# Rotated query halves by ScalarE row copies, and positional scores as split products on stacked rows

## The chip, the cores and the metric

The kernel runs on one core of one Trainium2 chip. TensorE (PE in the profile) multiplies matrices and writes to PSUM; VectorE (DVE) and ScalarE (ACT) do the elementwise work; GpSimd (POOL) and SyncE (SP) hardly compute here, and SP issues nearly all transfers. The metric is device microseconds for one execution of the whole kernel, the median of several runs. All numbers are float32 in memory.

## The reference

Two encoder layers over 256 tokens of width 2048. Each layer has two groups of attention heads that share one input projection, an output projection, and an MLP. This case touches the second group, multi-head latent attention with 8 heads. A head's query and key have a content part of 128 columns and a positional part of 64, and the positional key is the same for all heads:

```python
def _rope(x, cos, sin):
    half = x.shape[-1] // 2
    x1, x2 = x[..., :half], x[..., half:]
    out = jnp.concatenate([x1 * cos - x2 * sin, x2 * cos + x1 * sin], axis=-1)
    return out.astype(x.dtype)
...
        q_rope = _rope(q[..., MLA_NOPE:], cos[:, :, None, :], sin[:, :, None, :])
...
        k_rope = _rope(kr, cos, sin)
...
        s = (jnp.einsum('bhqd,bhkd->bhqk', qn, knt)
             + jnp.einsum('bhqr,bkr->bhqk', qr, k_rope)).astype(jnp.float32) * scale
        p = jax.nn.softmax(s, axis=-1)
        return jnp.einsum('bhqk,bhkd->bhqd', p.astype(vt.dtype), vt)
```

A rotation needs each 64-column vector twice: as it is, and with its two halves of 32 exchanged.

## The kernel before

Activations lie transposed, features on the 128 rows (partitions) and the 256 tokens along the free dimension. A weight comes from memory as a "raw" tile, 1 MB at a time, and is split into a high part in the format float32r (`hi`, made by ScalarE, line 151) and the remainder (`lo`, a subtraction on VectorE, line 154). A product is then three float32r matmuls: high by high, high by low, low by high (`mac`, lines 191 to 198). Smaller products, among them all scores, are plain float32 matmuls, each of which the profile shows as two instructions.

A layer of attention (function `layer`, lines 867 to 1018) emits its work in this order: the combined projection; the differential heads' columns, mixed with their probabilities (`probs`); `up_k`, the latent keys; `up_q(0)`, the content queries of heads 0 to 3; `up_r`, the positional queries of all heads; `mla[0]`, the scores of head 0; `up_v`, the latent values; the scores of head 1 and the transpose of head 0; `up_q(1)`; and then, interleaved, the value columns of the differential heads (`val`, whose matmuls are lines 296 to 298) with the other latent heads: scores, transpose, values, each head one step behind the last. The output projection `w_o` follows.

`up_r` (line 924) makes two PSUM banks, each with four heads' positional queries: two pairs of heads side by side along the free dimension, and the two heads of a pair on rows 0 to 63 and 64 to 127. `copy` (line 346) moves a bank to the tile `qr`, scaled. `rope_q` (line 1218) then exchanges the halves of 32 rows by a product with a permutation matrix (128 columns of the constants `K`, at `C_PERM`), into the bank `pqr`, and combines both with cosine and sine on VectorE (lines 1225 to 1227). `rope_k` (line 1203) makes the positional key once a layer: the tile `kr` holds it twice, on rows 0 to 63 of its first half and on rows 64 to 127 of its second, with zeros elsewhere (a GpSimd memset, line 1212), so that one float32 product of all 128 rows picks out one head of the pair. `scores` (lines 1310 to 1321) runs, for each of two blocks of 128 tokens, a content product (line 1315) and a positional product (line 1316) into the bank `psm`; VectorE negates it and finds the extreme (line 1317), ScalarE takes the exponentials (line 1236) and scales by the reciprocal sum (line 1320).

What sets the order: the program's order is a priority only. A scheduler orders each engine's instructions when the kernel is built, by that priority and its own estimate of when operands and buffers will be ready; on the chip each engine then goes through its list in order. `behind` adds an order by hand where a line asks for it; none of the touched lines does. The pools bound the distance: 5 raw buffers, 4 each of `hi` and `lo`, 40 tiles of 128x512 in the pool `u`, 6 in the pool `t`, 8 PSUM banks. Beside all this run the modulation weights (`ada`): 192 tiles of 1 MB, loaded into raw buffers at a set rate and reduced by VectorE (line 380).

Of the kernel before, what the change touches and what calls it, by code (L numbers as in the profile page):

```python
# [9 lines left out]
F32 = mybir.dt.float32  # L10
F32R = mybir.dt.float32r
I32 = mybir.dt.int32
AF = mybir.ActivationFunctionType
ALU = mybir.AluOpType
AX = mybir.AxisListType

P = 128
# [20 lines left out]
]  # L38

C_DELTA = 0  # L40
C_PERM = 32
C_CB = 160
C_W2 = 168
C_FREQ = 176
C_SGN = 177
C_ONE = 178
NCONST = 180

V_BADA = 0
V_SUBLN = 192  # L50
# [19 lines left out]
def consts():  # L70
    c = np.zeros((P, NCONST), np.float32)
    p = np.arange(P)
    c[p, C_DELTA + p % 32] = 1.0
    c[p, C_PERM + (p ^ 32)] = 1.0
    for g in range(8):
        for r in range(4):
            b = 4 * g + r
            n = b % 16
            lo, hi = BUCKET_FROM[n], BUCKET_FROM[n + 1] - 1
            sign = -1.0 if b < 16 else 1.0  # L80
            rows = slice(32 * r, 32 * r + 32)
            if b == 16:
                c[rows, C_CB + g], c[rows, C_W2 + g] = 0.0, -1.0
            else:
                c[rows, C_CB + g] = -sign * (lo + hi) / 2.0
                c[rows, C_W2 + g] = ((hi - lo) / 2.0 + 0.25) ** 2
    c[:, C_ONE : C_ONE + 2] = 1.0
    c[:32, C_ONE + 1] = 0.0
    c[:, C_FREQ] = np.asarray(INV_FREQ, np.float32)[p % 32]
    c[:, C_SGN] = np.where(p % 64 < 32, -1.0, 1.0)  # L90
    return c
# [10 lines left out]
class Trunk:  # L102
# [308 lines left out]
    def setup(self):  # L411
# [8 lines left out]
        nc.gpsimd.memset(self.eps, EPS)  # L420
        self.K = cp.tile([P, NCONST], F32, name="K")
        nc.sync.dma_start(self.K, io["consts"])
# [119 lines left out]
    def bias_marks(self, a):  # L542
# [5 lines left out]
        for g in (2, 3, 6, 7, 0, 1, 4, 5):  # L548
            sq = self.t("sq")
            self.by_act.append(nc.scalar.activation(sq, r, AF.Square, bias=K[:, C_CB + g : C_CB + g + 1]))  # L550
            oh = half("oh", F32R)
            flat = sq.rearrange("p a b -> p (a b)")
            if g % 4 < 2:
                c = C_ONE + (g == 4)
                self.by_act.append(nc.scalar.activation(oh, flat, AF.Relu, bias=K[:, c : c + 1], scale=-1.0))
            else:
                w2 = K[:, C_W2 + g : C_W2 + g + 1]
                self.by_dve.append(nc.vector.tensor_scalar(oh, flat, w2, None, ALU.is_le))
# [20 lines left out]
    def rope_setup(self):  # L579
# [3 lines left out]
        self.behind(nc.vector.tensor_copy(ang, pos[:, :T]), self.last_mod)  # L583
        nc.vector.tensor_scalar(ang, ang, K[:, C_FREQ : C_FREQ + 1], None, ALU.mult)
        magic = 1.5 * 2.0**23
# [15 lines left out]
        nc.scalar.activation(self.cos, c, AF.Sin)  # L601
        nc.vector.tensor_scalar(self.sin, self.sin, K[:, C_SGN : C_SGN + 1], None, ALU.mult)

# [263 lines left out]
    def layer(self, l, acc=None):  # L867
        nc, io = self.nc, self.io
        qs = 1.0 / math.sqrt(128.0)
        ms = 1.0 / math.sqrt(192.0)  # L870
# [29 lines left out]
        cq, ckv = [], []  # L900
        kk, qn, kn, qr, vm, a, at, v, o = [], [], [], [], [], [], [], [], []
# [20 lines left out]
            qn.extend(self.copy(ps, "qn", ms) for ps in self.small(io["w_uq"][l, b], cq, 4))  # L922

        def up_r():
            raw = [self.copy(ps, "qr", ms) for ps in self.small(io["w_uq"][l, 2], cq, 4)]
            qr.extend(self.rope_q(x) for x in raw)

        def up_v():
            w = self.weights(io["w_uv"][l])
# [54 lines left out]
        up_q(0)  # L984
        turn(0)()
        up_r()
        turn(1)()
        mla[0]()
# [24 lines left out]
        o = self.mo + o  # L1013
# [11 lines left out]
        for fb in range(NFB):  # L1025
            hid = []
            done = 12 - 6 * l
            for m in range(0 if fb else done, NK, 2):
                srcs = [io[f"w_m1{l}"][NK * fb + m + j - done] for j in range(2)]
                ps = self.wides(srcs, h)  # L1030
# [172 lines left out]
    def rope_k(self, ps):  # L1203

        nc = self.nc
        t = self.t("krt")
        for i in range(2):
            s = slice(64 * i, 64 * i + 64)
            nc.vector.tensor_tensor(t[s, 0], ps[:64], self.cos[:64], ALU.mult)
            nc.vector.tensor_tensor(t[s, 1], ps[64:], self.sin[:64], ALU.mult)  # L1210
        out = self.u("kr")
        nc.gpsimd.memset(out, 0.0)
        for i in range(2):
            s = slice(64 * i, 64 * i + 64)
            nc.vector.tensor_tensor(out[s, i], t[s, 0], t[s, 1], ALU.add)
        return out

    def rope_q(self, raw):
        nc = self.nc
        ps = self.bank("pqr")  # L1220
        flat = lambda x: x.rearrange("p a b -> p (a b)")
        nc.tensor.matmul(flat(ps), self.K[:, C_PERM : C_PERM + P], flat(raw), start=True, stop=True)
        t = self.t("qrt")
        wide = lambda x: x.unsqueeze(1).broadcast_to([P, 2, T])
        nc.vector.tensor_tensor(t, ps, wide(self.sin), ALU.mult)
        nc.vector.tensor_tensor(raw, raw, wide(self.cos), ALU.mult)
        nc.vector.tensor_tensor(raw, raw, t, ALU.add)
        return raw


    def softmax_parts(self, s, least):
# [74 lines left out]
    def mla_steps(self, hm, qn, qr, kn, vm):  # L1306
        nc = self.nc
        st = {}

        def scores():  # L1310
            ps = self.bank("psm")
            s, mx = self.t("sm"), self.s("mxm")
            for t in range(2):
                c = slice(t * P, (t + 1) * P)
                nc.tensor.matmul(ps[:, t], qn[hm // 2][:, hm % 2, c], kn[hm // 2][:, hm % 2], start=True, stop=False)
                nc.tensor.matmul(ps[:, t], qr[hm // 4][:, (hm // 2) % 2, c], self.kr[:, hm % 2], start=False, stop=True)
                nc.vector.tensor_scalar(s[:, t], ps[:, t], -1.0, None, ALU.mult, ALU.min, accum_out=mx[:, t : t + 1])
            r = self.softmax_parts(s, mx)
            for t in range(2):
                nc.scalar.activation(s[:, t], s[:, t], AF.Copy, scale=r[:, t : t + 1])  # L1320
            st["s"] = s

        def turn():
            st["t"] = self.transposed(st["s"])

        def values():
            if hm % 2 == 0:
                self.pom = self.bank("pom")
            for kt in range(2):
                c = (hm % 4) * P  # L1330
                v = vm[hm // 4][kt].rearrange("p a b -> p (a b)")
                nc.tensor.matmul(self.pom[:, hm % 2], v[:, c : c + P], st["t"][:, kt], start=kt == 0, stop=kt == 1)
            if hm % 2:
                self.mo += self.split(self.pom, "mo", True)

        return scores, turn, values


# [21 lines left out]
def _layout(i):  # L1360
# [6 lines left out]
    posq = np.tile(pos.reshape(8, 32).T, (4, 1))[:, order]  # L1367
    a["pos"] = np.ascontiguousarray(np.concatenate([np.broadcast_to(pos, (P, T)), posq], 1))
    a["consts"] = consts()
    feat = lambda v, n: v.reshape(n, P).T  # L1370
    vec = [feat(f["b_ada"][l], 96) for l in range(2)]
# [58 lines left out]
```

## Time and profile before

| what | value |
|---|---|
| median of 3 runs | 2177.95 us (2177.39 to 2180.36) |
| the profiled execution | 2180.82 us, span 2178.8 us |
| granted TensorE clock, mean | 0.998 |
| instructions | 29359 |
| read from memory | 589.66 MB, 272 GB/s over the span |

The profile is of one execution. Its page gives busy times and shares by engine, the chain of work that ended last, and the costliest groups of instructions; the trace behind it gives the instructions in order of time, busy times by window, and what each engine waited for. Line numbers are those of the kernel. Durations of neighbours on one engine overlap somewhat, so where steps matter the chain in order of time is the better view: it gives each piece without its overlap. A group's row reads: line, engine, operation, what it writes from what it reads, shapes, count, then busy us and mean ns of one, then idle time before them and what ended most of it.

### The profile page before, as it was taken

The page shows a single profiled execution, that of the slowest core. Times are in us where ns is not written, and L with a number is a line of the kernel's source. Part 1 is how long each engine was busy: PE and PEld are TensorE (multiplying, and loading weights), DVE is VectorE, ACT ScalarE, POOL GpSimd, SP SyncE. Part 2 cuts the span into 40 slices and gives each one's busy share as a digit, 9 for nine tenths or more (in the row PEclk, how much of TensorE's full clock was granted, in tenths as well). Part 3 has the DMA queues.
Part 4 walks back from the last instruction along what each step waited for, and adds up shares of the span by engine and source line. Part 5 has one row for each costly group of instructions (what it writes and reads, how often), then busy time and mean ns, then how long its engine had stood idle before and what let it go on. Part 6 is the DMA issues. An engine that isn't in the chain of part 4 may idle for free.

```text
span 2178.8 us, 29359 instructions
## 1 busy us (share of the span) xinstructions
PE 2147.1 (99%) x11502; PEld 1860.6 (85%) x11502; DVE 1592.7 (73%) x2117; ACT 1143.1 (52%) x1725; POOL 6.8 (0%) x19
## 2 busy tenths in 40 slices
PE   7999999999999999999999999999999999999998
PEld 6899878898888888888889988888888888888886
DVE  7888878888688988888876876678555555555555
ACT  6555664565455355355454565546535534644643
POOL 0000000000000000000000000000000000000000
PEclk9999999999999999999999999999999999999999
DMA  9988889799888988888967665867655554555552
GB/s 385 423 339 328 329 337 336 274 339 338 322 321 323 351 315 332 312 335 320 336 223 278 254 222 217 288 223 262 245 194 179 207 194 174 193 206 181 193 195 95
DMA packets 87243, 594.75 MB, mean 273 GB/s; under 512 B 9857, under 2 KB 10305, under 8 KB 20289
## 3 DMA queue, kind: packets, MB, share of 16 engines
q1 hardware_dynamic: 85968, 587.08, 73.2%
q0 software_dynamic: 848, 5.28, 0.7%
q8 instruction: 90, 1.47, 0.3%
q10 hardware_dynamic: 288, 0.52, 0.1%
q14 instruction: 49, 0.39, 0.1%
HBM read 589.66 MB, written 3.18 MB: 272 GB/s over the span
## 4 chain that ended last, share of the span: by engine, by line
PE 94%; DVE 2%; DMA 2%; ACT 1%; issue 0%; SPq 0%; ACTq 0%
PE ps L217 19%; PE pr L314 13%; PE pr L311 13%; PE pr L312 13%; PE ps L220 10%; PE pk L260 3%; PE pk L284 2%; PE pk L194 2%; PE pk L198 2%; PE pk L197 2%; PE pv L296 1%; PE pv L297 1%; PE pv L298 1%; DMA raw<-in_w_o 1%; PE pk L281 1%; PE ps L197 1%
## 5 line engine op out<-in xcount | busy, mean ns | idle before, releaser
L154 DVE TENSOR_TENSOR lo<-raw,hi 128x1024 fp32r<-128x1024 f32 (+1 forms) x714 | 835.6, 1193 | 441.1 <-issue 221.1
L151 ACT ACTIVATE hi<-raw 128x1024 fp32r<-128x1024 f32 (+1 forms) x714 | 733.9, 1036 | 685.8 <-PE pr L312 368.1
L380 DVE SCALAR_TENSOR_TENSOR ada<-ada,cond 128x2048 f32<-128x2048 f32 x192 | 437.9, 2284 | 12.4 <-DMA ada<-in_w_ada 11.9
L217 PE MATMUL ps<-h,hi 128*128 128x512 f32 x1856 | 431.5, 390 | 0.0
L217 PEld LDWEIGHTS ps<-h,hi 128*128 128x128 f32 x1856 | 345.1, 188 | 69.5
L311 PE MATMUL pr<-hi,hid 128*128 128x512 f32 x1024 | 398.6, 389 | 0.0
L312 PE MATMUL pr<-hi,hid 128*128 128x512 f32 x1024 | 398.5, 389 | 0.0
L314 PE MATMUL pr<-lo,hid 128*128 128x512 f32 x1024 | 253.5, 389 | 0.0
L220 PEld LDWEIGHTS ps<-h,lo 128*128 128x128 f32 x1856 | 230.3, 192 | 4.5
L220 PE MATMUL ps<-h,lo 128*128 128x256 f32 x1856 | 231.7, 283 | 0.0
L314 PEld LDWEIGHTS pr<-lo,hid 128*128 128x128 f32 x1024 | 192.3, 188 | 39.9
L312 PEld LDWEIGHTS pr<-hi,hid 128*128 128x128 f32 x1024 | 192.3, 188 | 39.7
L311 PEld LDWEIGHTS pr<-hi,hid 128*128 128x128 f32 x1024 | 192.3, 188 | 39.6
L1192 ACT ACTIVATE sum<-ps 128x256 f32<-128x256 f32 x110 | 42.0, 383 | 114.7 <-PE ps L220 114.2
L194 PE MATMUL pk<-h,hi 128*128 128x256 f32 x320 | 90.4, 285 | 0.2 <-ACT h L705 0.2
L198 PE MATMUL pk<-h,lo 128*128 128x256 f32 x320 | 90.5, 283 | 0.0
L197 PE MATMUL pk<-h,hi 128*128 128x256 f32 x320 | 90.5, 283 | 0.0
L188 DVE TENSOR_TENSOR hid<-relu,hid 128x256 fp32r<-128x256 f32 x128 | 48.3, 420 | 49.6 <-ACT hid L187 49.6
L260 PE MATMUL pk<-hf,w 128*128 128x256 f32 x384 | 83.9, 379 | 0.0
L260 PEld LDWEIGHTS pk<-hf,w 128*128 128x128 f32 x384 | 72.7, 190 | 10.0 <-ACT hf L677 0.2
L194 PEld LDWEIGHTS pk<-h,hi 128*128 128x128 f32 x320 | 61.2, 192 | 0.6 <-ACT h L705 0.5
L198 PEld LDWEIGHTS pk<-h,lo 128*128 128x128 f32 x320 | 61.4, 192 | 0.2 <-DVE lo L154 0.2
(237 smaller groups left out, 2466.6 us busy)
## 6 DMA issues: line engine op xcount, KB each, us to landing
raw<-in_w_m SPq DMA_DIRECT2D x238, 1024.0 KB, 5.2
ada<-in_w_ada SPq DMA_DIRECT2D x192, 1024.0 KB, 6.3
raw<-in_w_o SPq DMA_DIRECT2D x32, 1024.0 KB, 6.7
raw<-in_w_m SPq DMA_DIRECT2D x24, 768.0 KB, 5.6
raw<-in_w_dv SPq DMA_DIRECT2D x16, 1024.0 KB, 5.0
raw<-in_w_t SPq DMA_DIRECT2D x12, 1024.0 KB, 4.9
w<-in_w_a SPq DMA_DIRECT2D x24, 384.0 KB, 13.5
raw<-in_w_a SPq DMA_DIRECT2D x12, 768.0 KB, 5.8
```

Of the source, the lines that this page charges most:

```text
L151: ins = self.nc.scalar.activation(hi, v, AF.Copy)
L154: ins = self.nc.vector.tensor_tensor(lo, v, hi.bitcast(F32), ALU.subtract)
L194: ins = mm(ps, hi, x[0], start=first, stop=False, skip_group_check=shared)
L197: mm(ps, hi, x[1], start=False, stop=False, skip_group_check=shared)
L198: self.last_mac = mm(ps, lo, x[0], start=False, stop=last, skip_group_check=shared)
L217: mm(ps.rearrange("p a b -> p (a b)"), part(w, k, 0), x[2], start=k == 0, stop=False)
L220: mm(ps[:, 0], part(w, k, 1), x[0], start=False, stop=k == nk - 1)
L260: self.nc.tensor.matmul(ps, v, whole[k], start=first, stop=last, skip_group_check=True)
L311: mm(ps, xh[:, c], part(i, 0), start=kq == 0 and i == 0, stop=False)
L312: mm(ps, xl[:, c], part(i, 0), start=False, stop=False)
L314: self.last_mm = mm(ps, xh[:, c], part(i, 1), start=False, stop=kq == 3 and i == 3)
L380: ins = nc.vector.scalar_tensor_tensor(w, w, 1.0, self.cond, ALU.mult, ALU.mult, accum_out=acc[:, i : i + 1])
```

## The change

The permutation product is gone, and its constants with it. `up_r` hands the PSUM bank itself to `rope_q`, once for each bank as soon as it is made. `rope_q` makes the scaled copy as before, and the exchanged one by four ScalarE copies of 32 rows each from PSUM to the neighbouring 32 rows. After the rotation it splits the result into high and low parts and stacks them: one tile for each head of the pair, with the head's 64 high rows at their place and its 64 low rows at the other 64. The key is made in the same form: first half of `kr` the high part, second half the low part, on both sets of 64 rows, without zeros. A positional score is then two float32r products over 128 rows, (high + low) by high and (high + low) by low, in place of one float32 product.

```diff
 C_DELTA = 0
-C_PERM = 32
-C_CB = 160
...
-NCONST = 180
+C_CB = 32
...
+NCONST = 52
...
-    c[p, C_PERM + (p ^ 32)] = 1.0
...
         def up_r():
-            raw = [self.copy(ps, "qr", ms) for ps in self.small(io["w_uq"][l, 2], cq, 4)]
-            qr.extend(self.rope_q(x) for x in raw)
+            qr.extend(self.rope_q(ps, ms) for ps in self.small(io["w_uq"][l, 2], cq, 4))
...
             nc.vector.tensor_tensor(t[s, 0], ps[:64], self.cos[:64], ALU.mult)
             nc.vector.tensor_tensor(t[s, 1], ps[64:], self.sin[:64], ALU.mult)
-        out = self.u("kr")
-        nc.gpsimd.memset(out, 0.0)
+        both = self.t("krb")[:, 0]
         for i in range(2):
             s = slice(64 * i, 64 * i + 64)
-            nc.vector.tensor_tensor(out[s, i], t[s, 0], t[s, 1], ALU.add)
+            nc.vector.tensor_tensor(both[s], t[s, 0], t[s, 1], ALU.add)
+        out = self.u("kr", F32R)
+        nc.scalar.activation(out[:, 0], both, AF.Copy)
+        nc.vector.tensor_tensor(out[:, 1], both, out[:, 0].bitcast(F32), ALU.subtract)
         return out
 
-    def rope_q(self, raw):
-        nc = self.nc
-        ps = self.bank("pqr")
-        flat = lambda x: x.rearrange("p a b -> p (a b)")
-        nc.tensor.matmul(flat(ps), self.K[:, C_PERM : C_PERM + P], flat(raw), start=True, stop=True)
-        t = self.t("qrt")
+    def rope_q(self, ps, scale):
+
+        nc = self.nc
+        raw = self.copy(ps, "qr", scale)
+        rot = self.t("qrr")
+        for i in range(4):
+            j = i ^ 1
+            nc.scalar.activation(rot[32 * i : 32 * i + 32], ps[32 * j : 32 * j + 32], AF.Copy, scale=scale)
         wide = lambda x: x.unsqueeze(1).broadcast_to([P, 2, T])
-        nc.vector.tensor_tensor(t, ps, wide(self.sin), ALU.mult)
+        nc.vector.tensor_tensor(rot, rot, wide(self.sin), ALU.mult)
         nc.vector.tensor_tensor(raw, raw, wide(self.cos), ALU.mult)
-        nc.vector.tensor_tensor(raw, raw, t, ALU.add)
-        return raw
+        nc.vector.tensor_tensor(raw, raw, rot, ALU.add)
+        out = []
+        for i in range(2):
+            both = self.u("qrs", F32R)
+            s, o = (slice(64 * j, 64 * j + 64) for j in (i, 1 - i))
+            nc.scalar.activation(both[s], raw[s], AF.Copy)
+            nc.vector.tensor_tensor(both[o], raw[s], both[s].bitcast(F32), ALU.subtract)
+            out.append(both)
+        return out
...
-                nc.tensor.matmul(ps[:, t], qr[hm // 4][:, (hm // 2) % 2, c], self.kr[:, hm % 2], start=False, stop=True)
+                rope = qr[hm // 4][hm % 2][:, (hm // 2) % 2, c]
+                nc.tensor.matmul(ps[:, t], rope, self.kr[:, 0], start=False, stop=False)
+                nc.tensor.matmul(ps[:, t], rope, self.kr[:, 1], start=False, stop=True)
```

More of the change, by code (lines that the diff above doesn't have):

```diff
@@ L40 @@
 C_DELTA = 0
-C_PERM = 32
-C_CB = 160
[L43 to L46, printed above, removed]
-NCONST = 180
+C_CB = 32
+C_W2 = 40
+C_FREQ = 48
+C_SGN = 49
+C_ONE = 50
+NCONST = 52
 V_BADA = 0
```

## The prediction

> **What bounds the kernel now.** I read the page first (busy shares, the chain that ended last), then the change's own stretches by windows, then the timeline and the chain in order of time inside them.
>
> ```profile
> PE 2147.1 (99%) x11502; PEld 1860.6 (85%) x11502; DVE 1592.7 (73%) x2117; ACT 1143.1 (52%) x1725; POOL 6.8 (0%) x19
> PE 94%; DVE 2%; DMA 2%; ACT 1%; issue 0%; SPq 0%; ACTq 0%
> ```
>
> TensorE (PE) is busy 2147.1 of 2178.8 us and owns 94% of the chain. So a matmul taken away is worth its step, provided the next matmul has its operands. Whether it has is read from the stretches of the attention. The rotated queries are made near 220 us (layer 0) and 1280 us (layer 1); the positional scores follow for some 60 us.
>
> ```profile
> core 0: us, PE busy (x) PEld busy (x) DVE busy (x) ACT busy (x) POOL busy (x), PEclk, DMA share, GB/s
> 218.00:240.00 22.00, 21.40 (x133) 18.19 (x132) 21.59 (x35) 15.87 (x30) 0.00 (x0) 1.00 0.92 343
> 240.00:288.00 48.00, 48.00 (x225) 40.16 (x225) 40.08 (x64) 26.38 (x54) 0.00 (x0) 1.00 0.87 319
> 1278.00:1300.00 22.00, 21.62 (x134) 18.36 (x133) 15.94 (x29) 14.34 (x28) 0.00 (x0) 1.00 0.56 196
> 1300.00:1352.00 52.00, 52.00 (x244) 43.06 (x243) 32.82 (x56) 30.14 (x60) 0.00 (x0) 1.00 0.60 222
> ```
>
> In the two 22 us stretches after the query rotation PE is nearly full (0.60 and 0.38 us idle), but the others are not far off: ScalarE (ACT) has 6.1 us free in layer 0 and 7.7 in layer 1, VectorE (DVE) only 0.4 in layer 0 and 6.1 in layer 1. The clock is granted in full throughout. Keep these four numbers: the change puts its new work exactly there. In the two later stretches PE is without a gap, and both helpers have room.
>
> **What PE gains.** The chain in order of time gives PE's steps without their overlap:
>
> ```profile
> 1264.94 0.12 PE pss L197
> ...
> 1280.92 1.97 PE pqr L1222 x4
> 1282.89 0.44 PE pt L1267 x4
> 1283.33 0.43 PE psm L1315 x2
> ...
> 1285.38 0.43 PE psm L1316 x2
> ```
>
> The permutation product goes: 1.97 us in layer 1 for both halves (each 512-column f32 product is two instructions), with its wait for the second raw copy inside. I take 2.0 for layer 0 too: 4.0 in all. A positional score (L1316) is one f32 product of 256 columns, two instructions, 0.43 us. In its place stand two products of 256 columns in split form; such a product, with its own weight load, steps by 0.12 us at L197. So 0.43 becomes 0.24: 0.19 saved, 16 times a layer (8 heads, 2 row blocks), 3.0 a layer, 6.1 in all. PE's gross gain is 4.0 + 6.1 = **10.1 us**.
>
> **What ACT and DVE get.**
>
> ```profile
> L346 ACT ACTIVATE aT<-pt 128x512 f32<-128x512 f32 x24 | 14.2, 592 | 12.5 <-PE pt L1267 12.5
> L572 ACT ACTIVATE bias<-pb 32x512 f32<-32x512 f32 x16 | 9.4, 588 | 0.4 <-PE pb L569 0.2
> 69.80 2.39 ACT L572 ACTIVATE bias<-pb 32x512 f32<-32x512 f32 x4
> L182 ACT ACTIVATE lath<-lt 128x512 fp32r<-128x512 f32 x6 | 3.6, 623 | 4.7 <-DVE lt L725 4.7
> L183 DVE TENSOR_TENSOR latl<-lt,lath 128x512 fp32r<-128x512 f32 x6 | 4.1, 687 | 0.4 <-ACT lath L182 0.4
> L1225 DVE TENSOR_TENSOR qrt<-pqr,sin 128x512 f32<-128x512 f32 x4 | 2.7, 682 | 0.0
> L1226 DVE TENSOR_TENSOR qr<-qr,cos 128x512 f32<-128x512 f32 x4 | 2.7, 682 | 0.0
> L187 ACT ACTIVATE mo<-pom 128x256 fp32r<-128x256 f32 x16 | 6.1, 380 | 5.4 <-DVE mo L188 4.4 <-PE pom L1332 1.1
> L188 DVE TENSOR_TENSOR mo<-pom,mo 128x256 fp32r<-128x256 f32 x16 | 6.7, 419 | 4.8 <-ACT mo L187 4.6
> L1215 DVE TENSOR_TENSOR kr<-krt x4: 418/420/422, 158.8 to 1221.7; 64x256 f32<-64x256 f32 x4
> ```
>
> A copy of 32 rows from PSUM to other rows is already in the kernel (L572): 588 ns, no less than 128 rows (592), and four in a row take 2.39 us. So each of the two query halves gets 2.39 us of ACT work that the product did not need. Splitting into two stacked tiles adds two 64-row ACT copies; no row shows 64, so I bound them by the 32-row 0.59 and the 128-row 0.62 and take 0.6 (the rows count for nothing here). ACT gets 2 x 2.39 + 4 x 0.6 = **7.2 us a layer**. DVE's three rotation operations stay; the sine product reads SBUF instead of PSUM, and 682 beside 682 says that this is free. Four 64-row subtractions are added, bounded by 0.42 (L188, half the columns) and 0.69 (L183, the same columns, so my value): 2.7 us a layer, with no row that shows a different row start for output and inputs in SBUF.
>
> [...]
>
> Keys: one ACT copy (0.38) and one subtraction (0.42) more, two half additions and a memset moved or gone. The last key rows are written from 1221.7 us on (L1215) and first read at 1285 (below): 63 us cover it, and nothing is charged. The constants shrink from 180 to 52 columns, 66 KB in one early load; I count nothing. One PSUM bank a half is freed (pqr), and the raw bank is held about 2.4 us longer. Queues of SP and POOL gain nothing; POOL loses two memsets.
>
> **What of it lies on the path.** ACT's 7.2 us meets 6.1 and 7.7 free. This is the order in layer 1:
>
> ```profile
> 1278.08 0.60 ACT L346 ACTIVATE qr<-pss 128x512 f32<-128x512 f32 x1 [0.20 <-PE pss L198]
> 1280.17 1.06 ACT L151 ACTIVATE hi<-raw 128x1024 fp32r<-128x1024 f32 x1 [1.49 <-PE pss L197]
> 1281.13 0.58 ACT L346 ACTIVATE qr<-pss 128x512 f32<-128x512 f32 x1
> 1281.61 1.05 ACT L151 ACTIVATE hi<-raw 128x1024 fp32r<-128x1024 f32 x1
> 1281.26 1.23 DVE L154 TENSOR_TENSOR lo<-raw,hi 128x1024 fp32r<-128x1024 f32 x1
> 1283.41 0.58 PE L296 MATMUL pv<-hi,lath 128*128 128x512 f32 x1
> 1285.22 0.59 PE L1316 MATMUL psm<-kr,qr 128*128 128x256 f32 x2
> 1292.30 0.33 PE L1267 MATMUL pt<-ident,sm 128*128 128x128 f32 x1 [0.38 <-ACT sm L1320]
> ```
>
> The raw copy of the first half ends near 1278.6; ACT's next 1.49 us are idle and take part of the first four copies, the rest goes to 1281.0. Queued behind them on ACT: the split of the value weights (L151), for which PE waits next, then the softmax exponentials and the split for the second query product. The first value split ends at 1282.0 instead of 1281.2, the low part near 1283.2 or, behind the first rotation on DVE (three of 0.68), near 1284. PE, rid of the product, is through the transposes and the first content score at 1281.6. So it waits there for 1.6 to 2.4 us: the product's 2.0 us turns into a wait for the split. The first positional score needs the copies (1281.0), three DVE operations, an ACT copy and a subtraction, 3.3 us: 1284.3, before 1285.2 as now. The second half's copies push the second value split to about 1285 and its low part to 1287 or 1288, and the value products cover that; the scores inside the stretch (4 a layer, 0.76 us) are taken up by ACT's backlog, as the wait of 1292.30 on the softmax already shows ACT late there. I take the stretch as **even**, with -1.5 to +2 us a layer. In layer 0 ACT is short by 1 us and DVE, with 0.4 free, by 2.3; the same value, with more to lose.
>
> After the stretch, 12 scores a layer run in a PE without gaps: 12 x 0.19 = 2.3 us, kept in layer 1. In layer 0 PE soon meets this:
>
> ```profile
> 289.15 0.45 PE pt L1267 x4
> ...
> 294.65 5.76 DMA raw<-in_w_o
> ...
> 306.13 8.14 DMA raw<-in_w_o
> 310.00:320.00 10.00, 8.48 (x39) 6.37 (x38) 8.22 (x11) 6.97 (x16) 1.04 (x2) 1.00 0.98 374
> ```
>
> PE idles 1.52 us at 310 to 320, behind a chain through the loads of the output weights, while the DMA engines are 98% busy. The first of these loads was issued after work that PE had timed (a transpose at 289 us), so most of the gain moves through it; between 0 and 2.3 us, I take 2.2. Sum: 0 + 0 + 2.3 + 2.2 = **-4.5 us**. The profiled execution took 2180.82 us (span 2178.8 and 2.0 around it), 2.87 above the median of 2177.95; the sum is a difference, so it goes off the median: 2173.4.
>
> **The rivals.** A, the cover holds: the scheduler puts the value splits ahead of the copies, as they fit the idle 7.7 us of layer 1. Then 7.5 to 10.1 us stay, 2168 to 2170.5. For it: ACT is 52% busy over the span. Against: the copies stand earlier in the program, and DVE is full in layer 0.
>
> B, the gain is lost in layer 0: the loads of w_o arrive when they did, and the stretch costs 1 to 2 us a layer. -2 to +3: 2176 to 2181.
>
> C, slower: ACT runs both halves' copies before the first value split. It then ends at 1278.1 + 2 x (0.60 + 2.39) + 1.06 = 1285.1 instead of 1281.2, and the low part at 1286.4 instead of 1282.5: 3.9 us late, 1.9 more than the product freed; a split copy that waits for DVE's sum blocks ACT further. If all of ACT's addition lands on PE, 14.4 - 10.1 = +4.3, and with DVE's 5.4 up to +9.7. It decides from 5.1 us of new waits a layer: 2182 to 2187.
>
> [...]
>
> D, split products are hardly cheaper, because each shows its weight load:
>
> ```profile
> L197 PEld LDWEIGHTS pss<-latl,hi 128*128 128x128 f32 x128 | 24.5, 191 | 0.1
> ```
>
> A pair then costs 0.38 instead of 0.43, and 24 scores save 1.2, with 0 from the stretch: 2176.7. Against it: L197 steps by 0.12 with these very loads.
>
>
> **Chances.** Forecast (-6.5 to -2.5) 0.50, A 0.16, B 0.19, C 0.11, D 0.04. A measurement of this kernel tells about 0.2% (4.4 us) from no change. The forecast straddles that: 0.27 of it counts as faster, 0.23 as same. Faster 0.27 + 0.16 = 0.43; same 0.23 + 0.19 + 0.04 = 0.46; slower 0.11. The range 2169 to 2180 leaves out C, the last fifth of B and the best quarter of A.
>
> **What would show it.** Right: L1316's successors step by 0.12; the four copies take 2.4 us; PE idle in the two stretches grows by about 2 us each, ended by L151 or L154 of the value weights; 12 scores later nothing is idle in layer 1. Wrong: PE idle there stays under 1 us (A) or passes 5 us (C); the gap at 310 to 320 grows by the 2.3 us (B); steps of 0.2 (D). An order changed elsewhere could add 1 or 2 us that none of these terms holds.

## The result, and the profile after

The changed kernel takes 2185.81 us (median of 8 runs, 2183.17 to 2186.97), the kernel before beside it 2180.0 us (8 runs). The ratio is 1.0027, with a 95% interval of 1.0016 to 1.0038: slower by about 6 us, where 4.5 us less was forecast. The profiled execution has a span of 2185.1 us (before: 2178.8) and a granted clock of 0.996 (0.998).

The busy shares and the chain of the page, after:

```profile
PE 2143.6 (98%) x11494; PEld 1858.8 (85%) x11494; DVE 1598.8 (73%) x2127; ACT 1157.3 (53%) x1751; POOL 5.7 (0%) x17
PE 91%; DVE 4%; DMA 3%; ACT 1%; issue 0%; SPq 0%; ACTq 0%
```

TensorE has less to do and owns less of the chain: 94% became 91, and VectorE's part grew from 2 to 4%. The four windows of the prediction, and what TensorE waits for (us in total, times, longest), in the whole span and between 200 and 300 us:

```profile
218.00:240.00 22.00, 14.20 (x81) 11.40 (x80) 20.54 (x31) 16.78 (x28) 0.00 (x0) 0.99 0.72 253
240.00:288.00 48.00, 48.00 (x250) 41.28 (x251) 39.52 (x65) 31.96 (x67) 0.00 (x0) 0.97 0.82 307
1278.00:1300.00 22.00, 17.82 (x112) 15.78 (x112) 20.58 (x37) 20.93 (x37) 0.00 (x0) 0.95 0.66 230
1300.00:1352.00 52.00, 52.00 (x267) 44.59 (x266) 30.32 (x57) 31.07 (x64) 0.00 (x0) 0.96 0.60 219
```

```profile
PE psm L1323 <- DVE sm L1327: 8.6, 2, 4.4
...
PE psc L1257 <- DVE mx L1258: 2.3, 2, 1.7
PE psm L1323 <- ACT qrr L1224: 2.1, 1, 2.1
```

In the two stretches TensorE was idle 0.60 and 0.38 us; now it is idle 7.8 and 4.2. In the later windows it has no gap, as before. The long waits are none of those forecast (the splits of the value weights): on the low part of a value weight (L152 for L295) TensorE waits 0.3 us in layer 0, in layer 1 not at all. L1323 is the content product of a latent head's scores, L1327 the VectorE reduction of such scores. In both kernels a head's two blocks of 128 tokens share one PSUM bank, and in both traces the second block's content product starts, for all 8 heads of both layers, 0.47 us or more after VectorE began the reduction of the first block (0.40 to 0.43 us long). This is what stood in VectorE's and ScalarE's queues ahead of that reduction in layer 1 (timeline, in order of time):

```profile
1292.65 1.99 ACT L149 ACTIVATE hi<-raw 128x1024 fp32r<-128x1024 f32 x2
1293.39 0.69 DVE L1228 TENSOR_TENSOR qr<-qr,qrr 128x512 f32<-128x512 f32 x1
1294.00 1.22 DVE L152 TENSOR_TENSOR lo<-raw,hi 128x1024 fp32r<-128x1024 f32 x1
1294.54 1.27 ACT L1233 ACTIVATE qrs<-qr 64x512 fp32r<-64x512 f32 x2
1295.25 1.40 DVE L1234 TENSOR_TENSOR qrs<-qr,qrs 64x512 fp32r<-64x512 f32 x2
1296.68 1.23 DVE L152 TENSOR_TENSOR lo<-raw,hi 128x1024 fp32r<-128x1024 f32 x1
1297.90 0.40 DVE L1327 TENSOR_SCALAR_CACHE_REDUCE sm<-psm 128x256 f32<-128x256 f32 x1
1298.37 1.22 PE L1323 MATMUL psm<-kn,qn 128*128 128x256 f32 x2 [4.17 <-DVE sm L1327]
```

Head 1's first block was scored at 1294.0. VectorE took it up only at 1297.90 and was busy until then: ahead stood the subtractions of the second query half (L1234, 1.40 us, for heads 4 to 7, while TensorE was at head 1) and the low parts of the next weights (L152, 1.22 and 1.23 us). In the kernel before, the same reduction came between these two low parts:

```profile
1290.40 1.23 DVE L154 TENSOR_TENSOR lo<-raw,hi 128x1024 fp32r<-128x1024 f32 x1 [0.94 <-ACT hi L151]
...
1291.95 0.42 DVE L1317 TENSOR_SCALAR_CACHE_REDUCE sm<-psm 128x256 f32<-128x256 f32 x1 [0.25 <-PE psm L1316]
...
1294.60 1.23 DVE L154 TENSOR_TENSOR lo<-raw,hi 128x1024 fp32r<-128x1024 f32 x1 [0.40 <-ACT hi L151]
```

So of the 3.9 us 1.4 are new work, and 1.2 are a low part that the new order put in front. TensorE stood idle in front of L1323 for 4.17 us.

The wait has a second price. The granted clock (last number but two) in three windows around it:

```profile
1294.00:1297.40 3.40, 0.19 (x2) 0.00 (x0) 3.31 (x5) 3.34 (x7) 0.00 (x0) 1.00 0.70 282
1297.60:1304.30 6.70, 5.93 (x26) 5.76 (x27) 3.51 (x10) 5.03 (x13) 0.00 (x0) 0.51 0.80 290
1304.50:1308.00 3.50, 3.50 (x31) 3.50 (x30) 0.00 (x0) 1.13 (x2) 0.00 (x0) 1.00 0.07 30
```

After the gap TensorE runs at half clock (0.51) for 6.7 us (products step by 0.21 instead of 0.12 us). It is busy for 5.93 of them, so this costs about 2.9 us more.

The ledger: take the same TensorE instruction in both traces and subtract its start times. Layer 0 and layer 1 then show where the time came in:

| stretch | shift after minus before, us | gained or lost |
|---|---|---|
| at 60 us | +0.6 | +0.6 |
| to 235 us (layer 0, scores of heads 0 and 1) | +8.7 | +8.1 |
| to 300 us (other heads) | +6.8 | -1.9 |
| to 600 us (output projection, MLP) | +4.6 | -2.2 |
| to 1295 us (layer 1, the same scores) | +8.7 | +4.1 |
| to the end (other heads) | +6.5 | -2.2 |

### The profile page after: what moved, and what is told of

The parts are those of the page before. It is cut to its first block, busy times and chain, and to the rows that moved or that the text cites. A ratio compares the mean times of both kernels' runs of the same rounds, so it can differ in the third digit from the quotient of the medians.

```text
span 2185.1 us, 29376 instructions
## 1 busy us (share of the span) xinstructions
PE 2143.6 (98%) x11494; PEld 1858.8 (85%) x11494; DVE 1598.8 (73%) x2127; ACT 1157.3 (53%) x1751; POOL 5.7 (0%) x17
## 4 chain that ended last, share of the span: by engine, by line
PE 91%; DVE 4%; DMA 3%; ACT 1%; issue 0%; SPq 0%; ACTq 0%
PE ps L215 19%; PE pr L309 13%; PE pr L310 13%; PE pr L312 13%; PE ps L218 10%; PE pk L258 3%; PE pk L282 2%; PE pk L192 2%; PE pk L196 2%; PE pk L195 2%; PE pv L294 1%; PE pv L296 1%; PE pv L295 1%; DMA ada<-in_w_ada 1%; PE pk L279 1%; DVE lo L152 1%
## 5 line engine op out<-in xcount | busy, mean ns | idle before, releaser
L152 DVE TENSOR_TENSOR lo<-raw,hi 128x1024 fp32r<-128x1024 f32 (+1 forms) x714 | 836.3, 1194 | 445.0 <-issue 217.4
L149 ACT ACTIVATE hi<-raw 128x1024 fp32r<-128x1024 f32 (+1 forms) x714 | 733.4, 1036 | 685.1 <-PE pr L310 364.4
```

Source lines behind the costliest of these rows:

```text
L149: ins = self.nc.scalar.activation(hi, v, AF.Copy)
L152: ins = self.nc.vector.tensor_tensor(lo, v, hi.bitcast(F32), ALU.subtract)
```

## The experiments

Four theories stood at the outset: **order** (the second half's rotation and splits stand ahead of head 0's and 1's softmax), **occupancy** (7.2 us more for ScalarE, 2.7 for VectorE do not fit the stretch), **bank** in the sense of the copies holding the raw bank (2.1 us, L1224 in the rows above), and **key** (the key's two more operations shift layer 0 before the queries). All runs have five rounds against the kernel before. For each, the table gives the median, the ratio with its interval, and what the ledger shows for layer 0 (between 60 and 600 us) and layer 1 (1100 to 2000 us). The layers come from one execution each, and it need not be a typical one: e17's was the fastest of its 11 (2171.31 us), e18's the slowest of its 7 (2174.78 us). Layer 1 repeats (e12, e13, e14, e17, e18: -6.2 or -6.3); in layer 0 the ledger is coarser, since all reordered kernels gain 1 to 2 us on the profiled execution of before in the output projection.

| run | edit | us | ratio (95%) | layer 0 | layer 1 |
|---|---|---|---|---|---|
| the change | | 2185.81 | 1.0027 (1.0016 to 1.0038) | +4.0 | +1.9 |
| e1 | copies read SBUF | 2188.37 | 1.0044 (1.0031 to 1.0057) | +6.2 | +3.2 |
| e2 | e1, second half late | 2183.35 | 1.0018 (1.0009 to 1.0027) | +3.3 | -1.8 |
| e3 | product back, split scores | 2183.11 | 1.0020 (1.0011 to 1.0030) | +2.6 | -1.2 |
| e4 | copies, float32 scores | 2181.03 | 1.0007 (0.9998 to 1.0016) | +1.9 | -2.4 |
| e5 | queries exchanged | 2191.90 | 1.0058 (1.0045 to 1.0071) | +3.1 | +7.6 |
| e6 | rotation before keys | 2182.56 | 1.0014 (1.0006 to 1.0023) | -1.9 | +2.5 |
| e7 | e2, no modulation there | 2192.37 | 1.0068 (1.0054 to 1.0081) | +13.7 | -1.7 |
| e8 | head 0's scores later | 2189.65 | 1.0048 (1.0036 to 1.0061) | +5.2 | +4.0 |
| e9 | reductions behind both blocks | 2179.47 | 1.0006 (0.9997 to 1.0015) | +2.4 | -4.3 |
| e10 | e2 and e9 | 2179.34 | 1.0002 (0.9993 to 1.0011) | +3.2 | -4.2 |
| e11 | before, with e9's order | 2178.54 | 0.9997 (0.9988 to 1.0006) | -2.3 | -1.2 |
| e12 | e10, differential heads too | 2177.64 | 0.9995 (0.9986 to 1.0003) | +3.5 | -6.2 |
| e13 | e12 in layer 1 only | 2171.98 | 0.9967 (0.9954 to 0.9979) | -3.9 | -6.2 |
| e14 | e12, modulation earlier | 2179.27 | 0.9997 (0.9988 to 1.0006) | +6.3 | -6.3 |
| e15 | before, with e12's order | 2176.72 | 0.9987 (0.9978 to 0.9995) | -3.9 | -2.1 |
| e16 | the change, with e12's order | 2176.83 | 0.9995 (0.9986 to 1.0004) | -0.4 | -4.1 |
| e17 | e12, layer 0's first half early | 2173.93 | 0.9974 (0.9966 to 0.9983) | -3.2 | -6.3 |
| e18 | e12, layer 0's halves early | 2173.39 | 0.9972 (0.9961 to 0.9983) | -0.1 | -6.2 |

### e1 to e4: one part of the change at a time

e1, the exchanged copies read the raw copy in SBUF:

```diff
-            qr.extend(self.rope_q(ps, ms) for ps in self.small(io["w_uq"][l, 2], cq, 4))
+            raw = [self.copy(ps, "qr", ms) for ps in self.small(io["w_uq"][l, 2], cq, 4)]
+            qr.extend(self.rope_q(x) for x in raw)
...
-            nc.scalar.activation(rot[32 * i : 32 * i + 32], ps[32 * j : 32 * j + 32], AF.Copy, scale=scale)
+            nc.scalar.activation(rot[32 * i : 32 * i + 32], raw[32 * j : 32 * j + 32], AF.Copy)
```

> The exchanged copies read the raw copy in SBUF instead of the PSUM bank, so each bank is free after its raw copy; all else is as in the changed kernel (2185.8 us). Bank theory: the 2.05 us in layer 0 in which a score product waits for the last exchanged copy go, the two waits of 4.2 and 4.4 us stay: about 2183.8. Order theory (the second half's rotation and splits stand ahead of head 0's and 1's softmax on ScalarE and VectorE): the same, or up to 2186 if the next thing late takes the place. Occupancy theory (ScalarE's 7.2 us more a layer are simply too much for the stretch): no change, 2185 to 2187.

e2, the same and the second half's rotation later:

```diff
-            qr.extend(self.rope_q(x) for x in raw)
+            qr.append(self.rope_q(raw[0]))
+            return raw[1]
...
-        up_r()
+        second = up_r()
...
         turn(3)()
+        qr.append(self.rope_q(second))
         for f in mla[3:6]:
```

> As e1, and the second half's exchanged copies, rotation and splits stand in the program after the second content queries, behind the scores of heads 0 and 1; the same instructions otherwise, none left out. Order theory: the waits of 2.05, 4.4 and 4.2 us and most of the clock lost behind them go, 8 to 11 us: 2175 to 2178. Occupancy theory: the same work still has to be done in the same 22 to 30 us, the waits move by a few instructions: 2183 to 2187.

e3 has `rope_q` of the kernel before up to the rotated result, then the splits of the change; keys and scores of the change:

```diff
-        rot = self.t("qrr")
-        for i in range(4):
...
+        ps = self.bank("pqr")
+        flat = lambda x: x.rearrange("p a b -> p (a b)")
+        nc.tensor.matmul(flat(ps), self.K[:, C_PERM : C_PERM + P], flat(raw), start=True, stop=True)
```

> Rotation by the permutation product as before, keys and scores in split form as in the changed kernel: eight exchanged copies fewer on ScalarE (4.8 us a layer), 2.0 us a layer more on TensorE. Occupancy theory: ScalarE keeps 2.4 us of the 7.2, the waits of 10.6 us go nearly all: 2185.8 - 10.6 + 4.0 = 2179, or 2176 if no other wait comes. Order theory: the second half's splits and subtractions still stand ahead of the reductions; each wait shrinks by at most the 2.4 us of a half's copies and TensorE pays 4.0: 2184 to 2188. Key theory: the 3 us that come in at 195 to 215 us of the span stay.

e4 has the copies, but the key and the scores of the kernel before:

```diff
-        out = []
-        for i in range(2):
-            both = self.u("qrs", F32R)
...
-        return out
+        return raw
...
-                nc.tensor.matmul(ps[:, t], rope, self.kr[:, 0], start=False, stop=False)
-                nc.tensor.matmul(ps[:, t], rope, self.kr[:, 1], start=False, stop=True)
+                nc.tensor.matmul(ps[:, t], qr[hm // 4][:, (hm // 2) % 2, c], self.kr[:, hm % 2], start=False, stop=True)
```

> Rotation by ScalarE copies as in the changed kernel, key and scores in float32 as before: no splits of queries and keys (2.4 us of ScalarE and 2.8 of VectorE a layer fewer), 3.0 us a layer more on TensorE. Order theory: the subtractions that held VectorE's queue are gone, so the 4.4 and 4.2 us fall to 1 us or less, and the score products give 6.1 back: 2181 to 2184, or 2179 to 2181 if the key's extra operations are what costs 3 us at 195 to 215 us. Occupancy theory: 4.8 of ScalarE's 7.2 us stay, half or more of the waits stay: 2185 to 2190.

The waits of TensorE in e1 (200 to 300 us) and e2 (timeline, layer 0 twice, layer 1), then e3's in both layers:

```profile
PE psm L1323 <- DVE sm L1327: 4.3, 2, 4.0
PE psm L1325 <- DVE qrs L1234: 3.4, 1, 3.4
```

```profile
231.72 0.39 PE L1327 MATMUL psm<-kr,qrs 128*128 128x256 f32 x1 [3.35 <-DVE qrs L1236]
...
237.46 0.79 PE L1325 MATMUL psm<-kn,qn 128*128 128x256 f32 x1 [3.69 <-DVE sm L1329]
...
1295.35 0.70 PE L1325 MATMUL psm<-kn,qn 128*128 128x256 f32 x2 [2.17 <-DVE sm L1329]
```

```profile
238.49 0.79 PE L1324 MATMUL psm<-kn,qn 128*128 128x256 f32 x1 [3.67 <-DVE sm L1328]
...
1296.57 0.70 PE L1324 MATMUL psm<-kn,qn 128*128 128x256 f32 x2 [2.27 <-DVE sm L1328]
```

e1 missed: the wait for the copies goes, but a wait of 3.4 us for the first split query comes, as both raw copies now precede the exchanged ones. Holding the raw bank isn't what costs the rest; since e1 also changed the order of the copies, it doesn't show what those 2.1 us were worth alone. By their times, e2 (2183.35) lies where occupancy put it and e3 (2183.11) where no theory did; e4 (2181.03) lies where the order theory did. The layers say more. In layer 1 all three agree with the order: with the second half late the wait is 2.2 instead of 4.2 us and the clock stays full (1.00 from 1284 to 1304 us; 3.7 us gained), with fewer copies in the queue 2.3, and with no splits none: there the product's 2.0 us come through whole, so eight copies by themselves are hidden in layer 1. What is left of the wait in e2 has nothing of the second half in front of it: VectorE stands 1.16 us idle at head 0's reciprocal, which waits for ScalarE's exponentials, and head 1's reduction comes behind that. In layer 0 all four lose 1.9 to 6.2 us, even e4, where TensorE waits 2.87 us before the first positional product; there the order doesn't suffice. In e4 the shift at 195 to 210 us is gone (+0.1 instead of +4.4 us), so the key's operations do reorder that place. By 230 us the changed kernel is back at about +0.3, but this holds what it doesn't pay on the way: the 2.12 us that the kernel before waits for weights at 214 us, and the product's 2.0. So a part of the key's delay may remain; no run takes the key's operations away alone.

### e5 to e8: more distance, less occupancy

e5:

```diff
-        up_q(0)
+        up_r()
         turn(0)()
-        up_r()
+        up_q(0)
```

> The changed kernel with the positional queries made before the content queries of heads 0 to 3 (their places in the program exchanged): 5.8 us of TensorE products more between the rotation and the first score. Distance theory (what is late is the chain raw copy, four copies, three VectorE operations, split, and what queues behind it on ScalarE and VectorE; the work itself would fit): the waits of 2.05, 4.4 and 4.2 us with the slow clock behind them shrink by half or more: 2174 to 2180. Occupancy theory (ScalarE and VectorE have no room between 218 and 245 us of the span, and 1284 to 1300): nothing is gained by a few us of distance, 2183 to 2187.

e6:

```diff
+        up_r()
         up_k()
         probs(3)()
...
-        up_r()
```

> The changed kernel with the positional queries made before the latent keys, some 15 to 20 us earlier, where VectorE and ScalarE stand at 65 and 52 per cent in the kernel before (196 to 220 us of the span). Distance and occupancy theories alike: the waits in both stretches go and the products' 10.1 us come through, 2169 to 2175. If it stays above 2180, neither is the cause, and it lies in the scores themselves (order of the score products, bank, softmax).

e7, on top of e2:

```diff
+        if l == 0:
+            self.rate = 0.0
         up_q(0)
...
-            self.rate = RATE_V
+            self.rate = RATE_V + 0.55
```

> e2 (second half late), and in layer 0 no modulation weights are loaded during the query and value products (some four reductions of 2.3 us on VectorE less between 218 and 240 us; they come later). Occupancy theory for layer 0 (VectorE is full of these reductions there): the waits of 3.35 and 3.69 us in layer 0 and the slow clock behind them go, 6 to 9 us: 2174 to 2178. Distance theory: the chain of copies, rotation and split is as long as before, 1 to 3 us less: 2180 to 2183. Layer 1 as in e2.

e8:

```diff
-        mla[0]()
         up_v()
+        mla[0]()
```

> The changed kernel with the scores of head 0 moved in the program behind the latent values' products. Distance theory: the first score no longer stands between rotation and values; the waits fall by half or more, 2175 to 2181. Occupancy theory: 2183 to 2187. If the wait of head 1 on head 0's VectorE reductions (4.4 and 4.2 us) only moves on, it is the chain of softmax behind the second half's subtractions: 2184 to 2188.

The rows of e5 (timeline, layer 1), e6 (waits, layer 1) and e8 (waits, whole span) follow.

```profile
1295.43 1.22 PE L1323 MATMUL psm<-kn,qn 128*128 128x256 f32 x2 [11.10 <-ACT qn L344]
```

```profile
PE psm L1323 <- ACT qn L344: 2.6, 1, 2.6
```

```profile
PE psm L1323 <- DVE sm L1327: 13.0, 3, 6.5
```

Both simple theories fell: e5 and e8 are slower than the changed kernel, and e6 (2182.56 us) is above 2180, where its expectation called neither the cause. In e5 and e6 the content queries' copies now stand on ScalarE behind the rotation, and TensorE waits for them, 11.1 and 2.6 us. In e8 the first score is out of the way, and the waits for L1327 grow to 6.5 and 6.3 us: the third outcome that its expectation names, the reductions behind the second half's subtractions. e7 bears occupancy out for the stretch of layer 0: VectorE has no modulation reduction between 218 and 240 us, where e2 has five, the two waits shrink from 3.35 and 3.69 to 0.54 and 1.23 us, and its shift is 0.0 at 240 us, where e2's is +6.3. But the modulation weights put off come back between 280 and 380 us, where the last value weights and the output weights are loaded, and cost 14 us.

### e9 to e12: the shared bank

From here on, "bank" in the expectations means the score bank that the two blocks of a head share. The same line is added in the scores of the latent heads of the changed kernel (e9), of e2 (e10) and of the kernel before (e11); e12 is e10 with such a line in `diff_probs` as well:

```diff
             for t in range(2):
                 c = slice(t * P, (t + 1) * P)
                 nc.tensor.matmul(ps[:, t], qn[hm // 2][:, hm % 2, c], kn[hm // 2][:, hm % 2], start=True, stop=False)
...
+            for t in range(2):
                 nc.vector.tensor_scalar(s[:, t], ps[:, t], -1.0, None, ALU.mult, ALU.min, accum_out=mx[:, t : t + 1])
```

> The changed kernel, but a latent head's six score products (both blocks of 128 tokens) stand ahead of its two VectorE reductions; nothing else. Bank theory: the 4.38 and 4.17 us are the second block's content product waiting for the reduction of the first block, which shares its PSUM bank; with the reductions behind, TensorE doesn't wait for VectorE inside a head, and the two waits with most of the slow clock behind them go: 8 to 14 us, 2172 to 2178. Pure distance or occupancy theory: TensorE needs the softmax a step later anyway (transposes), the wait moves there and at most 3 us are saved: 2182 to 2186.

> e2 (second half late, copies from SBUF) with the same order of products and reductions. Bank theory: e2's waits of 3.69 and 2.17 us go and the 3.35 us for the first split query stays: 2183.35 - 6 to 9 = 2174 to 2178. Distance or occupancy theory: 2181 to 2184.

> The kernel before with the same order of products and reductions: it shows how much of the gain of e9 belongs to the order alone. The kernel before has 0.55 and 0.38 us idle in the two stretches, so there is little to gain: 2178 to 2180.5 by every theory; lower would mean that this order is worth something by itself.

> e10, and the differential heads' score products of both blocks also ahead of their two reductions (they wait 0.64 and 1.69 us at 205 to 208 us of the span in all kernels with the split key). Bank theory: 2 us less than e10, with the slow clock of 3.4 us behind it up to 4: 2171 to 2176. Otherwise as e10.

TensorE's waits in layer 1 (1230 or 1270 us on) in e9 and e12, one row each, and the longest in layer 0 (200 to 300 us) in e9:

```profile
PE pss L192 <- ACT aT L344: 1.5, 1, 1.5
```

```profile
PE psm L1328 <- DVE qrs L1236: 0.5, 1, 0.5
```

```profile
PE pt L1275 <- ACT sm L1331: 3.7, 1, 3.7
```

One line, no instruction more or less, takes the changed kernel from 1.0027 to 1.0006, some 4.6 us (6.3 by the medians, which come from different sittings). In layer 1 the 4.17 us wait is gone with its slow clock (1.00 from 1278 to 1352 us), and the layer goes from +1.9 to -4.3 us. The kernel before gains 1.2 from the same line in layer 1, so 5 of these 6.2 us belong to the change's own wait. In layer 0 the wait mostly moves, as the rival theories expected: head 1's second block no longer waits 4.38 us, but head 0's transposes wait 3.74 us for its softmax. So for the change the order is shown as the cause in layer 1, not in layer 0. e9, e10 and e12 all ended 1 to 2 us above the times that the bank theory gave. e12 also loses the 0.63 and 1.69 us of the differential heads (L1257), without a gain in layer 0 (+3.5 us, e10 +3.2). Layer 0 still loses 2.4 to 3.5 us.

The runs show that the 4.17 us go with the order; why a product waits for the reduction of the bank's other half, they do not show.

### e13 to e18: layer 0, and a version that beats both

e13, on e12 (`rope_k32` and `rope_q32` are the functions of the kernel before):

```diff
-            self.kr = self.rope_k(ps[:, 0])
+            self.kr = (self.rope_k if l else self.rope_k32)(ps[:, 0])
...
+            if l == 0:
+                qr.extend(self.rope_q32(x) for x in raw)
+                return
...
+                if not isinstance(qr[0], list):
+                    nc.tensor.matmul(ps[:, t], qr[hm // 4][:, (hm // 2) % 2, c], self.kr[:, hm % 2], start=False, stop=True)
+                    continue
```

> e12 in layer 1 alone; layer 0 keeps the rotation by product, the float32 positional scores and the zero-padded key of the kernel before (with the reductions behind the products of both blocks). If the bank explains layer 1 and layer 0 loses by the change: layer 0 gives -1 to -2 as in e11, layer 1 -5 to -6.3 as in e12: 2171 to 2174. If layer 1's gain depends on what layer 0 leaves behind: 2175 to 2178.

e14, on e12:

```diff
-        if l:
-            self.rate = RATE_A2
+        self.rate = RATE_A2 if l else 2.2
         up_k()
...
+        if l == 0:
+            self.rate = 0.0
         second = up_r()
```

> e12 with the modulation loads of layer 0 paid earlier: rate 2.2 instead of 1.1 during the keys' and the content queries' products, none during the rotation and the latent values. If VectorE's reductions are what costs layer 0: the 2.69 us before the value products at 224 us go, 2 to 4 us: 2174 to 2176. If it is the loads of the output weights at 290 to 400 us (3.10 us idle at 368): 2177 to 2180.

e15 is the kernel before and e16 the changed kernel, each with the reductions behind both blocks in the latent and the differential heads.

> The kernel before, with latent and differential heads' reductions behind the products of both blocks (e11 and its counterpart): the baseline for e16 and e12. The kernel before waits little on these: 2177 to 2179.

> The changed kernel in the same order as e15, second half not moved. Bank theory: most of e12's gain in layer 1 without moving the second half, 2176 to 2180. If the place of the second half is what counts in layer 1: 2180 to 2184.

e17, on e12; e18 has `qr.append(self.rope_q(up_r()))` at the same place:

```diff
+        if l == 0:
+            second = up_r()
         up_k()
         probs(3)()
```

> e12 with layer 0's positional queries made before the latent keys (first half's rotation there, second half's late); layer 1 as in e12 (-6.25). Place theory: with the chain where VectorE has room, layer 0 gives what the products save there, 3 to 5 us less than e15's layer 0 at best: 2168 to 2172. If layer 0 has no place for it: 2174 to 2178.

> e17 with both halves of layer 0 rotated and split there. Place theory: the stretch at 218 to 240 us is then free of all added work, 2168 to 2172, below e17. If ScalarE's 7.2 us hold up the keys' and content queries' copies behind them, as the 2.65 us wait for a content query in e6: 2174 to 2179.

With the same order in both kernels the change is even: 2176.83 us (e16) beside 2176.72 (e15), and by the ledger the two layers nearly cancel (against e15, 3.5 us lost in layer 0 and 2.0 gained in layer 1). e13's layer 1 has one wait of 0.5 us and gives the same -6.2 us as e12's, whatever layer 0 does; the gain of layer 1 is its own. e13 is 7.0 us faster than before, and so faster than both kernels. What it has over e15 (4.7 us by the medians, 4.1 by the ledger in layer 1) is what the change is worth there when its order is right.

e14 only moves layer 0's loss: TensorE now waits for two splits of query weights, 3.51 us at 209 us and 2.90 us at 221 us; the load of the second was issued at 214.35 us, behind a modulation load, and its split started at 220.24. e17 shows where layer 0's chain goes when it is put into the room at 196 to 220 us (timeline, ScalarE):

```profile
208.11 1.29 ACT L1238 ACTIVATE qrs<-qr 64x512 fp32r<-64x512 f32 x2 [2.09 <-DVE qr L1233]
...
209.42 2.07 ACT L344 ACTIVATE kn<-pss 128x512 f32<-128x512 f32 x4
...
214.16 1.99 ACT L149 ACTIVATE hi<-raw 128x1024 fp32r<-128x1024 f32 x2
```

ScalarE stands 2.09 us idle at its own split copy, which waits for VectorE's sum; the keys' copies, the exponentials and the next weight split (L149) queue behind it, and TensorE waits 4.30 us for that. The stretch behind is then good: from 60 to 300 us e17 gains 3.8 us, where e15 loses 0.2. It gives this back at one place of the output projection, between 360 and 370 us (e17, timeline, in order of time):

```profile
356.93 2.29 DVE L378 SCALAR_TENSOR_TENSOR ada<-ada,cond 128x2048 f32<-128x2048 f32 x1
...
360.59 0.63 ACT L1136 ACTIVATE sq<-x 128x512 f32<-128x512 f32 x1 [2.82 <-DVE x L1122]
...
361.22 1.99 ACT L149 ACTIVATE hi<-raw 128x1024 fp32r<-128x1024 f32 x2
...
362.31 0.80 PE L309 MATMUL pr<-hi,mo 128*128 128x512 f32 x1 [2.09 <-ACT hi L149]
```

Here a modulation reduction stands between the two halves of the sum of the output on VectorE; ScalarE's square waits for the second half, the split of an output weight stands behind the square, and TensorE waits for the split. With the rest behind it this costs e17 4.0 us (its shift goes from -4.8 to -0.8). e12 and e18 have a reduction at the same place and lose 3.4 and 4.0 us; e13, e15 and e16 have none there and lose nothing. At the end of the layer e17 and e18 therefore stand at -3.2 and -0.1, against e15's -3.9 without the change. By the medians of all runs e13, e17 and e18 can't be told apart.

## Why the prediction was wrong

**The sizes were right.** The changed kernel's groups, and two scores in the chain, in full clock:

```profile
L1224 ACT ACTIVATE qrr<-pss 32x512 f32<-32x512 f32 x16 | 9.4, 589 | 0.2
...
L1233 ACT ACTIVATE qrs<-qr 64x512 fp32r<-64x512 f32 x8 | 5.0, 626 | 0.2
...
L1234 DVE TENSOR_TENSOR qrs<-qr,qrs 64x512 fp32r<-64x512 f32 x8 | 5.5, 686 | 0.3
...
1308.71 0.43 PE psm L1323 x2
1309.14 0.12 PE psm L1325
1309.26 0.12 PE psm L1326
1310.25 0.64 PE psm L1323 x2
```

Copies 589 ns (588 taken), split copies 626 (600), subtractions 686 (687), a positional score 0.24 us (0.24). The permutation product's 2.0 us show in the ledger of e13 as -2.0 between 1275 and 1280 us, the twelve later scores as -1.9 and -2.2 (2.3 taken). Rival D (split products hardly cheaper) is out.

**The failed step is "I take the stretch as even".** It priced the change by sums: ScalarE's 7.2 us against 6.1 and 7.7 free. The stretch came out at +8.1 and +4.1. Three things were missing. First, the place: the step followed the value weights' splits, and in layer 1 it took the wrong rows for them. These are rows of the changed kernel:

```profile
1279.97 1.04 ACT L149 ACTIVATE hi<-raw 128x1024 fp32r<-128x1024 f32 x1
...
1286.44 0.40 PE L295 MATMUL pv<-lo,lath 128*128 128x512 f32 x1
...
1287.67 1.22 DVE L152 TENSOR_TENSOR lo<-raw,hi 128x1024 fp32r<-128x1024 f32 x1
```

The value products read a low part at 1286.44, while the low part of the split behind the copies (L149 at 1285.70) is made only at 1287.67. So the value weights had been split at 1278.51 and 1279.97, ahead of the copies, and the split behind them (1280.17 and 1281.61 in the kernel before) belongs to the second content queries. In layer 0 a value split does stand behind the first half's copies, but the change waits only 0.3 us for its low part. The forecast's wait (1.6 to 2.4 us for that split) shows in the reordered kernels, in layer 0: 1.91 us in e16 and 2.69 us in e12 (L294, for L149). What came late in the change was the reduction of a score block, behind work for heads 4 to 7 and the next weights. A row that pointed there was in reach. In the chain of before, in order of time, a first and a second block's content product:

```profile
1308.52 0.43 PE psm L1315 x2
...
1310.05 0.55 PE psm L1315 x2
```

The second block takes 0.12 us more: TensorE waited for VectorE inside a head even then (0.64 in the rows of after above; in e11, with the reductions behind both blocks, it is 0.43). Second, the clock, which added some 2.9 us to the 4.2 of the wait in layer 1. Third, layer 0's VectorE with 0.4 us free: this was seen ("DVE, with 0.4 free, by 2.3") and given "the same value" as layer 1. e7, without its modulation reductions, has the stretch nearly even.

**Rival C** (chance 0.11) had the sign and the time (2182 to 2187). Its threshold, new waits above 5.1 us a layer, was passed in layer 0 (7.2) and in layer 1 only with the lost clock (3.8 and some 2.9). Its mechanism isn't what happened: the value splits weren't late, and what blocked was the order on VectorE in front of the softmax. Its further term, a split copy that waits for DVE's sum, comes to no more than 0.2 us of idle ScalarE in the change (L1233 in the rows above), and to 2.09 us at one place of e17. So its time is right in part by luck. **Rival B** fell for the change: layer 0 gave back 2.2 us of its delay in the output projection instead of swallowing a gain. Its kind exists: e12 is at +0.4 us at 360 us and at +3.8 at 370, with 3.10 us idle before an output-weight product, and e17 loses its gain there, to a reduction's place more than to a load. **Rival A**, the cover, comes true in layer 1 once the order is right: the value splits stand ahead of the copies there, as it said, and 4.1 of 5.05 us come through (e13 against e15).

Keys "charged nothing" is not settled (see e4). "An order changed elsewhere could add 1 or 2 us" was true in kind (the differential heads' waits, 2.3 us) and small beside the rest.

What stays open is layer 0. In the change its stretch has waits for the copies, the split queries and the reductions (7.2 us), and e7 makes it even by taking VectorE's modulation reductions away. e12 makes it even by the order (+0.4 us at 215 and at 240 us), and e17 has a gain by 300 us; both then lose 3.4 to 4.0 us behind the reduction in the output projection. No run moves that reduction, so that layer 0 would then gain is not shown.

## What to carry over

When work is added to helper engines, don't compare its sum with the idle time of the stretch: write down each helper's list in program order and ask which instruction of the bound engine waits for one that now stands behind the new work, above all behind a new instruction that itself waits. Work that is not needed soon belongs behind work that is. Where TensorE fills two halves of a bank and a helper empties them, put both products first; one line made the same instructions of the changed kernel some 4.6 us cheaper here, and those of the kernel before hardly (ratio 0.9997).

## What the hardware showed that was not expected

A wait of TensorE can cost more than its length (in layer 1 of the changed kernel 4.17 us, and then some 2.9 at a clock of 0.51), and not by a fixed length. These rows are the 4 us behind the same wait of 2.12 us for the same weights, in the kernel before and in e4 (windows; the clock is the last number but two):

```profile
214.00:218.00 4.00, 3.48 (x27) 3.27 (x28) 4.00 (x3) 0.90 (x1) 0.00 (x0) 1.00 0.21 31
```

```profile
214.00:218.00 4.00, 3.90 (x18) 3.71 (x19) 3.92 (x3) 0.99 (x2) 0.00 (x0) 0.59 0.26 33
```

The one keeps the full clock (1.00), the other falls to 0.59. In the changed kernel half clock is granted from 1297.6 to 1304.3 us in layer 1 (0.51, shown above) and twice for some 3.3 us in layer 0 (0.50 and 0.52):

```profile
208.80:212.10 3.30, 3.30 (x18) 3.30 (x17) 3.30 (x6) 2.50 (x4) 0.00 (x0) 0.50 0.11 17
...
239.40:242.70 3.30, 2.91 (x11) 2.73 (x12) 3.30 (x8) 3.30 (x9) 0.00 (x0) 0.52 0.67 273
```

So 2.12 us of waiting were followed by a slow clock in e4 and not in the kernel before; no run shows what decides it.
